# Layer 0's attention: latent before context, and two heads' value products in turn

## The chip, the core and the metric

The kernel runs as one program on one core of a Trainium2 chip. The time is that of the device, in microseconds (us): 2790.97 before the change, the median of three runs (2787.93 to 2791.73). TensorE (PE in the rows) multiplies matrices, VectorE (DVE) and ScalarE (ACT) do the elementwise work, and the queue of SyncE (SP) issues the transfers from the device's memory. Each engine takes its instructions in one fixed order that is set when the program is built.

## The reference, cut to what matters

The model is a trunk of four layers over 256 latent and 256 context tokens with 1024 features. Each layer has a token mixer and a squared-ReLU MLP. The change is in layer 0's mixer, multi-head latent attention with 16 heads. Keys and queries have 96 features per head, values 64:

```
q, k, v = project(u, True)          # 256 latent tokens
qc, kc, vc = project(uc, False)     # 256 context tokens
k_all = jnp.concatenate([k, kc], axis=2)
v_all = jnp.concatenate([v, vc], axis=2)
o  = softmax(q  k_all^T * scale) v_all     # latent queries see 512 keys
yc = softmax(qc kc^T    * scale) vc        # context queries see the 256 context keys
```

## The kernel before

The activations lie with features on partitions and 512 tokens (latent, then context) along the row. The function `mla_heads` works on heads in pairs, eight pairs one after another. The two heads of a pair fill the two halves of one output tile: head `e` = 0 goes to partitions 0 to 63 and head 1 to partitions 64 to 127 of `out`, a PSUM tile named `st`.

For one head there are four query tiles of 128 tokens: two latent ones that see 512 keys, and two context ones that see 256. One query tile is a *unit* in what follows:

- L864, TensorE: the score product `sc` = queries x keys.
- `softmax` (L664 to L667): VectorE takes the maximum (L664) and scales it (L665), ScalarE takes the exponential (L666), VectorE the reciprocal of the sum (L667).
- L868, VectorE: the probabilities `p` are scaled.
- L871, TensorE: `p` is transposed in blocks of 128 x 128 into `ax`.
- L879, VectorE and ScalarE: the transposed blocks are copied to `pt`, in which keys lie on partitions.

After its four units the head is multiplied with its values (L888): four products of 128 keys x 64 outputs x 256 latent queries, summed in one half of `out`, and then two for the context queries. All products of one head write the same half of the partitions; the other head's follow after its own four units. There are 16 x (4 + 2) = 96 such products. After both heads, `split` (L639, L640) cuts `out` into the two parts `uh` and `ul` that the output projection reads.

Between the units, `self.aside` takes steps of a generator: the projections of the next pair (`proj1` and `project`, whose products are L294 to L296 into `pj`), in the last pair the first products of the output projection (`early`). After each head, two steps of layer 0's modulation are made (`ada`, L432: four products with 32 output columns each, that write the four quarters of an `st` tile). The weights come through a ring of four buffers `raw` (L269 for weight blocks, L429 for the modulation), and ScalarE (L277) and VectorE (L278) split each weight block into `whi` and `wlo`.

The rows of buffers in `MLA_ROWS` give each kind of tile its ring: four buffers for `pt`. In which order instructions of one engine stand is settled by a scheduler when the program is built; a product in fp32 stands in the trace as two MATMUL records and two LDWEIGHTS records, a 128 x 128 transpose as one of each.

Of the kernel before, what the change touches and what calls it, by code (L numbers as in the profile page):

```python
# [12 lines left out]
F32 = mybir.dt.float32  # L13
# [8 lines left out]
S = 256  # L22
T2 = 512
# [19 lines left out]
MLA_ROWS = dict(q=4, k=4, p=4, pt=4, x=3)  # L43
# [4 lines left out]
class Cols:  # L48
    """Column layout of the packed per-feature parameters."""
# [19 lines left out]
def _wa(w, kc=8):  # L69
    """[K, F] -> [F/128, K/(128 kc), 128, kc * 128]: blocks that hold one tile of outputs."""  # L70
    k, f = w.shape
    w = w.reshape(k // (128 * kc), kc, 128, f // 128, 128)
    return np.ascontiguousarray(w.transpose(3, 0, 2, 1, 4)).reshape(f // 128, k // (128 * kc), 128, kc * 128)


def _wb(w):
    """[K, F] -> [F/512, K/256, 128, 2 * 512]: blocks that hold 512 outputs of 256 inputs."""
    k, f = w.shape
    w = w.reshape(k // 256, 2, 128, f // 512, 512)
    return np.ascontiguousarray(w.transpose(3, 0, 2, 1, 4)).reshape(f // 512, k // 256, 128, 1024)  # L80


def _rope(dim):
    """cos and signed sin of the axial positions: [128 features (whole heads), 256 tokens] each."""
# [10 lines left out]
def _layout(x):  # L95
    """Host side: arrays as the kernel reads them (transposed, cut and joined; no arithmetic)."""
# [40 lines left out]
    # rows 0-63 see (forward, backward) in the two passes over a token tile, rows 64-127 the other way round  # L137
# [18 lines left out]
class Trunk:  # L156
    def __init__(self, ctx, tc, ins, out):
        self.ctx, self.tc, self.nc, self.I, self.out = ctx, tc, tc.nc, ins, out
        # what a layer norm is cut into
# [32 lines left out]
    def open_acc(self, pool):  # L192
        """Banks for products in turn from a pool of two and from that for projections beside other work."""
        acc, pj = ("acc", pool("acc", 2, space=PSUM)), ("pj", self.pj)
        turn = cycle((acc, acc, pj, pj))

        def tile():
            n, p = next(turn)
            return p.tile([128, T2], F32, name=n)
        self.acc = tile  # L200

    def proj1(self, block, n=T2, kc=8, x=None, every=2):
        """As proj, for one block and from the pool for projections beside other work; yields after every few input tiles."""
# [20 lines left out]
    def after(self, ins, other):  # L224
        """ins comes after other, of the same engine."""
# [9 lines left out]
    def tables(self):  # L235
        """Loads the tables of exp and ln, both, after the last silu."""
# [5 lines left out]
    def weights(self, *key):  # L242
        """One block of weights, split; the blocks that come after it are loaded and split ahead."""
# [13 lines left out]
    def load(self, name, *at):  # L257
        """Loads one block of weights and splits it: hi + lo, both with at most 12 significant bits; some stay whole."""
# [13 lines left out]
    def halved(self, pool, src, n=""):  # L272
        """Up to 1024 columns from DRAM, split."""
# [7 lines left out]
    def blocks(self):  # L281
        """The blocks of weights in the order of their use."""
# [15 lines left out]
    def proj(self, blocks, n=T2, t0=0, kc=8, x=None, outer=None, spare=False):  # L298
        """Yields PSUM tiles [128 features, n tokens]; blocks: weight blocks, one per output tile.
        outer: output widths of blocks whose products go together, input tile by input tile.  # L300
        spare: the first product goes to another pool."""
# [32 lines left out]
    def ada_prepare(self):  # L334
# [3 lines left out]
        # stationary operands of 32 columns: both conditions, and sums of partitions into one column or the other  # L338
# [8 lines left out]
        # picks the streams' rows from each quarter, or their sums over the quarters  # L347
# [4 lines left out]
    def begin(self, raw, blocks):  # L352
        """The first sub-layer's input, tile by tile as its modulation arrives, and beside it the products with the
        first blocks of weights, which arrive between; returns those products."""
# [57 lines left out]
    def aside(self, n=None):  # L412
        """The next n steps of the modulation that is worked out beside other things."""
# [3 lines left out]
    def ada(self, i):  # L417
        """Modulation of layer i: mods[:, 8 * kind + tile, stream]; yields 8 times for each kind (begin makes the first two of
        layer 0).  The products of layer 0 are TensorE's, those of the others, which come beside an MLP, VectorE's."""
# [37 lines left out]
    def coef(self, i, sub, r):  # L457
        """u = n * A + B and the gate for layer i, sub-layer sub, stream r; n is -2 times the normalised stream, without gain."""
# [28 lines left out]
    def ln_add(self, d, a, b):  # L487
        """Takes columns a to b of tile d of z, complete (the first two tiles come with all their columns).
        Sums are about c, the mean of the features of the first two tiles; it is taken from the others beforehand."""
# [19 lines left out]
    def ln_finish(self, a, b):  # L509
        """Mean (of what is left of z) and -2 / deviation of columns a to b."""  # L510
# [11 lines left out]
    def rsqrt(self, out, x):  # L522
        """out = -2 (x + eps) ** -0.5: the tables' value and one Newton step; x is overwritten."""
# [15 lines left out]
    def coefs(self, i, sub, t=T2):  # L539
        """All that turns the normalised parts into the input of a sub-layer, and its gates."""  # L540
# [3 lines left out]
    def enter(self, sub, r):  # L544
        """u (split) and the residual of a sub-layer from stream r, normalised."""
# [21 lines left out]
    def last_tiles(self, blocks, x, kc, sub):  # L567
        """The last four output tiles before a layer norm, part by part: what follows it begins with one
        part while the other is still under way.  sub: what follows, or None at the end."""
# [22 lines left out]
    def last_part(self, sub):  # L592
        """What is left of a layer norm, to be made once the next sub-layer has begun."""
# [6 lines left out]
    def mlp(self, i, t, following=None):  # L600
        """following: makes the coefs of the sub-layer after it, which is entered."""
# [40 lines left out]
    def rsqrt_sum(self, out, s, n, t):  # L642
        """out = -2 (sum over partitions of s / n + eps) ** -0.5, on all partitions; s is overwritten."""
# [6 lines left out]
    def rope(self, x, swapped, tab, out):  # L650
        """x: [128, >= 256] in SBUF; swapped: scratch; out: list of (destination, partitions)."""
# [8 lines left out]
    def softmax(self, p, ps, n, scale):  # L660
        """p = exp(scale * ps - max); returns 1 / sum per partition."""
# [19 lines left out]
    def early(self, name, n=7):  # L681
        """The products of the first n input tiles with the first two blocks of an output projection."""
# [31 lines left out]
    # the order of the projections of the gated linear attention, after the first four  # L714
# [16 lines left out]
    # the order of the other projections of the gated delta rule, after the first keys  # L731
# [15 lines left out]
    def mixer0(self, i):  # L747
        nc, I = self.nc, self.I
        with ExitStack() as ctx:
# [9 lines left out]
            def gather(raw, blocks):  # L759
                """Copies of products and the sum of their squares."""  # L760
# [47 lines left out]
    def mla_heads(self, pool, vp, tab, cq, ck, kr):  # L808
# [7 lines left out]
        def project(quad):  # L816
            """Values of 4 heads, queries and keys of 2 pairs."""
# [32 lines left out]
        for pair in range(8):  # L850
# [6 lines left out]
            for e, (q, k) in enumerate(qk):  # L857
                hp = slice(64 * e, 64 * e + 64)
                pts = []
                for qt in range(4):  # L860
                    lat = qt < 2
                    k0, nk = (0, 4) if lat else (S, 2)
                    sc = self.sc.tile([128, T2], F32, name="sc")
                    nc.tensor.matmul(sc[:, :128 * nk], lhsT=q[0:96, 128 * qt:128 * qt + 128],  # L864
                                     rhs=k[0:96, k0:T2], start=True, stop=True)
                    p = row("p")
                    r = self.softmax(p, sc, 128 * nk, scale)
                    nc.vector.tensor_scalar_mul(p[:, :128 * nk], p[:, :128 * nk], r)  # L868
                    tp = self.ax.tile([128, T2], F32, name="ax")
                    for kt in range(nk):  # L870
                        nc.tensor.transpose(tp[:, 128 * kt:128 * kt + 128], p[:, 128 * kt:128 * kt + 128], self.ident)  # L871
                    if qt % 2 == 0:
                        pt = [row("pt") for _ in range(nk // 2)]
                        pts.append(pt)
                    # pt[j][:, kt % 2, query]
                    for j in range(nk // 2):
                        dst = pt[j].rearrange("p (k q) -> p k q", k=2)[:, :, 128 * (qt % 2):128 * (qt % 2) + 128]
                        src = tp[:, 256 * j:256 * j + 256].rearrange("p (k q) -> p k q", k=2)
                        (nc.scalar.copy if j else nc.vector.tensor_copy)(dst, src)  # L879
                    if pair == 7:  # L880
                        self.aside(2)
                    elif pair + 1 not in made:
                        self.aside(1 + pair % 2)
                h = 2 * (pair % 2) + e
# [983 lines left out]
```

## Time and profile before

| what | us |
|---|---|
| median of three runs | 2790.97 |
| lowest and highest run | 2787.93, 2791.73 |
| the profiled execution, first to last instruction | 2789.6 |
| TensorE busy | 2691.3 (96%) |
| VectorE busy | 2025.3 (73%) |
| ScalarE busy | 1255.1 (45%) |

The profiled execution is 1.4 us shorter than the median of the runs. A busy TensorE row counts the time in which at least one product is on its way; since products overlap, how long one holds the engine is read from the distance between the starts of two, not from its length.

### The profile page before, as it was taken

How to read it: one execution, taken by the hardware profiler on the slowest of the kernel's cores; microseconds unless marked ns; L12 is line 12 of the kernel's file. 1: busy time of each engine (PE TensorE's matmuls, PEld its weight loads, DVE VectorE, ACT ScalarE, POOL GpSimd, SP SyncE). 2: the span in 40 equal slices, each digit the busy share in tenths (PEclk: the TensorE clock that was granted, in tenths of full speed). 3: DMA queues.
4: the chain of work that ended last, by engine and by line, in shares of the span. 5: the costliest groups of instructions: out<-in, count | busy, mean ns of one | idle time of the engine just before them, and what ended most of it. 6: DMA issues, size and time to landing. Idle time of an engine off the chain costs nothing. (4 is left out here: it accounts for less than half of the span.)

```text
span 2789.6 us, 41018 instructions
## 1 busy us (share of the span) xinstructions
PE 2691.3 (96%) x15728; PEld 2166.6 (78%) x15728; DVE 2025.3 (73%) x3908; ACT 1255.1 (45%) x2413; POOL 47.9 (2%) x75
## 2 busy tenths in 40 slices
PE   7999999999999989999999999999999998998998
PEld 5666787788876687888888887887887876657997
DVE  3666798784757799875754489876689897668666
ACT  3544453333545663332454455322354555444544
POOL 0000000000000000000000000000000111000000
PEclk9999999999999999999999999999999898999999
DMA  6533237564121126654311125664322445313453
GB/s 232 174 97 104 78 106 218 180 191 134 59 69 50 34 79 218 197 175 147 93 63 56 58 76 178 199 189 159 117 82 81 158 153 151 107 29 121 159 182 113
DMA packets 125536, 353.26 MB, mean 127 GB/s; under 512 B 37499, under 2 KB 41339, under 8 KB 124828
## 3 DMA queue, kind: packets, MB, share of 16 engines
q1 hardware_dynamic: 121804, 337.00, 38.3%
q0 software_dynamic: 3536, 13.63, 1.3%
q8 instruction: 124, 2.03, 0.3%
q14 instruction: 72, 0.59, 0.1%
HBM read 335.91 MB, written 14.68 MB: 126 GB/s over the span
## 5 line engine op out<-in xcount | busy, mean ns | idle before, releaser
L277 ACT CAST whi<-raw 128x1024 fp32r<-128x1024 f32 (+2 forms) x403 | 410.4, 1023 | 694.0 <-PE acc L295 259.9
L278 DVE TENSOR_TENSOR wlo<-raw,whi 128x1024 fp32r<-128x1024 f32 (+2 forms) x403 | 478.0, 1189 | 199.7 <-ACT whi L277 193.9
L294 PE MATMUL pj<-ul,whi 128*128 128x512 f32 (+1 forms) x1072 | 398.6, 372 | 1.1 <-DVE z L565 1.0
L296 PE MATMUL pj<-uh,wlo 128*128 128x512 f32 (+1 forms) x1072 | 386.9, 361 | 0.6 <-DVE wlo L278 0.6
L295 PE MATMUL pj<-uh,whi 128*128 128x512 f32 (+1 forms) x1072 | 386.2, 360 | 0.0
L438 DVE SCALAR_TENSOR_TENSOR acc<-raw,s,acc 128x1024 f32<-128x1024 f32 x252 | 317.2, 1280 | 31.8 <-DMA raw<-in_ada 28.7
L294 PE MATMUL acc<-ul,whi 128*128 128x512 f32 (+3 forms) x888 | 311.7, 351 | 15.9 <-DVE ul L554 11.0
L295 PE MATMUL acc<-uh,whi 128*128 128x512 f32 (+3 forms) x888 | 308.7, 348 | 0.0
L296 PE MATMUL acc<-uh,wlo 128*128 128x512 f32 (+3 forms) x888 | 308.5, 347 | 0.0
L294 PEld LDWEIGHTS pj<-ul,whi 128*128 128x128 f32 x1072 | 203.0, 189 | 37.4 <-issue 6.3
L296 PEld LDWEIGHTS pj<-uh,wlo 128*128 128x128 f32 x1072 | 203.0, 189 | 32.6 <-issue 4.6
L295 PEld LDWEIGHTS pj<-uh,whi 128*128 128x128 f32 x1072 | 203.2, 190 | 30.1 <-issue 5.8
L294 PE MATMUL pj<-hl,whi 128*128 128x512 f32 (+1 forms) x560 | 198.3, 354 | 0.7 <-DVE hl L621 0.3
L294 PEld LDWEIGHTS acc<-ul,whi 128*128 128x128 f32 (+2 forms) x888 | 167.2, 188 | 40.6 <-DVE ul L554 12.9
L295 PE MATMUL acc<-hh,whi 128*128 128x512 f32 (+1 forms) x560 | 197.5, 353 | 0.0
L294 PE MATMUL acc<-hl,whi 128*128 128x512 f32 (+1 forms) x560 | 196.8, 351 | 0.0
L295 PE MATMUL pj<-hh,whi 128*128 128x512 f32 (+1 forms) x560 | 196.7, 351 | 0.0
L296 PE MATMUL acc<-hh,wlo 128*128 128x512 f32 (+1 forms) x560 | 196.5, 351 | 0.0
L296 PE MATMUL pj<-hh,wlo 128*128 128x512 f32 (+1 forms) x560 | 196.2, 350 | 0.0
L296 PEld LDWEIGHTS acc<-uh,wlo 128*128 128x128 f32 (+2 forms) x888 | 167.1, 188 | 22.1 <-issue 1.2
L295 PEld LDWEIGHTS acc<-uh,whi 128*128 128x128 f32 (+2 forms) x888 | 167.3, 188 | 20.8 <-issue 1.0
L620 ACT CAST hh<-t 128x512 fp32r<-128x512 f32 (+1 forms) x128 | 72.2, 567 | 123.6 <-DVE t L619 123.2
(463 smaller groups left out, 5001.0 us busy)
## 6 DMA issues: line engine op xcount, KB each, us to landing
raw<-in_w SPq DMA_DIRECT2D x256, 512.0 KB, 4.2
raw<-in_ada SPq DMA_DIRECT2D x192, 512.0 KB, 4.7
raw<-in_diff_qk SPq DMA_DIRECT2D x16, 512.0 KB, 3.5
raw<-in_gdn_v SPq DMA_DIRECT2D x16, 512.0 KB, 4.0
raw<-in_gdn_z SPq DMA_DIRECT2D x16, 512.0 KB, 4.5
raw<-in_gdn_out SPq DMA_DIRECT2D x16, 512.0 KB, 3.9
raw<-in_mla_in SPq DMA_DIRECT2D x9, 512.0 KB, 7.5
raw<-in_mla_qb SPq DMA_DIRECT2D x12, 384.0 KB, 3.6
```

The costliest lines, as they stand in the source:

```text
L277: nc.scalar.copy(hi[:, :width], raw[:, :width])
L278: nc.vector.tensor_sub(lo[:, :width], raw[:, :width], hi[:, :width].bitcast(F32))
L294: mm(ps, lhsT=ah, rhs=bl, start=start, stop=False)
L295: mm(ps, lhsT=ah, rhs=bh, start=False, stop=False)
L296: mm(ps, lhsT=al, rhs=bh, start=False, stop=stop)
L438: nc.vector.scalar_tensor_tensor(acc[r], w, self.s[:, k, r:r + 1], acc[r], op0=ALU.mult, op1=ALU.add)
L620: nc.scalar.copy(hh[:, f, :t], r[:, :t])
```

## The change

For each pair, the two latent query tiles of both heads are now taken first (query tile by query tile, both heads in turn), then the value products of both heads for the latent queries, then the same for the context. Within the value products, the key tiles follow each other, and for each key tile head 1 and head 0 are multiplied in turn. `pt` has six buffers in place of four, two per head for the latent and one for the context. Two steps of the modulation follow the latent and two the context, where two followed each head. Comments are left out as well, so that lines behind move: L871, L879 and L888 become L870, L875 and L884.

```
-MLA_ROWS = dict(q=4, k=4, p=4, pt=4, x=3)
+MLA_ROWS = dict(q=4, k=4, p=4, pt=6, x=3)
...
-            for e, (q, k) in enumerate(qk):
-                hp = slice(64 * e, 64 * e + 64)
-                pts = []
-                for qt in range(4):
-                    lat = qt < 2
-                    k0, nk = (0, 4) if lat else (S, 2)
...
-                h = 2 * (pair % 2) + e
-                for pt, o, t0 in ((pts[0], out[:, :S], 0), (pts[1], out[:, S:], 2)):
-                    nk = 2 * len(pt)
-                    for kt in range(nk):
-                        nc.tensor.matmul(o[hp], lhsT=v[:, t0 + kt, 64 * h:64 * h + 64],
-                                         rhs=pt[kt // 2][:, S * (kt % 2):S * (kt % 2) + S],
-                                         start=kt == 0, stop=kt == nk - 1)
+            for lat in (True, False):
+                k0, nk, t0, o = (0, 4, 0, out[:, :S]) if lat else (S, 2, 2, out[:, S:])
+                pts = [[row("pt") for _ in range(nk // 2)] for _ in qk]
+                for qt in range(2):
+                    qa = (0 if lat else S) + 128 * qt
+                    for (q, k), pt in zip(qk, pts):
...
+                for kt in range(nk):
+                    for e in (1, 0):
+                        h, pt = 2 * (pair % 2) + e, pts[e]
+                        nc.tensor.matmul(o[64 * e:64 * e + 64], lhsT=v[:, t0 + kt, 64 * h:64 * h + 64],
+                                         rhs=pt[kt // 2][:, S * (kt % 2):S * (kt % 2) + S], start=kt == 0, stop=kt == nk - 1)
                 for _ in islice(modulation, 2):
                     pass
```

In the built program the instructions are the same ones, and ahead of and behind this attention each engine's order is unchanged; the queues of SP and POOL are unchanged throughout. On TensorE 767 instructions in a row differ in their order. A first place is TensorE in the fourth pair, where the six value products of the first head stand before the change (`pt` and `v`: L888; `ident` and `p`: transposes; `raw` and `s`: the modulation):

```order
L888 MATMUL st<-pt,v 64x256 x2
L871 MATMUL ax<-ident,p 128x128 x2
L888 MATMUL st<-pt,v 64x256
L654 MATMUL ax<-x,swap 128x256
L888 MATMUL st<-pt,v 64x256 x3
L432 MATMUL st<-raw,s 32x256 x8
```

In the same pair after the change, TensorE has the latent products of both heads:

```order
L870 MATMUL ax<-ident,p 128x128 x4
L654 MATMUL ax<-x,swap 128x256
L296 MATMUL pj<-ck_132,wlo 128x512
L294 MATMUL pj<-cq_131,whi 128x512
L295 MATMUL pj<-cq_130,whi 128x512
L884 MATMUL st<-pt,v 64x256 x8
L432 MATMUL st<-raw,s 32x256 x8
L870 MATMUL ax<-ident,p 128x128 x2
```

Pieces of two, one and three products, all for the same half, became one piece of eight in which the halves alternate. A second place is ScalarE where two weight blocks of a later projection are split (`whi<-raw`), before the change:

```order
L879 COPY pt<-ax 128x2x128
L666 ACTIVATE p,sm<-sc,sm 128x256
L277 CAST whi<-raw 128x256
L666 ACTIVATE p,sm<-sc,sm 128x512
L277 CAST whi<-raw 128x768
L666 ACTIVATE p,sm<-sc,sm 128x512
```

And ScalarE at the same two weight blocks after the change:

```order
L666 ACTIVATE p,sm<-sc,sm 128x512
L666 ACTIVATE p,sm<-sc,sm 128x256
L277 CAST whi<-raw 128x256
L277 CAST whi<-raw 128x768
L875 COPY pt<-ax 128x2x128
L666 ACTIVATE p,sm<-sc,sm 128x256 x2
L447 COPY t_2181<-st 128x256
```

The two casts now stand next to each other, with a copy to `pt` and the exponentials of context units behind them.

## Rows read from the trace of the kernel before

**Rows 1.** The page: busy time, then busy tenths and granted clock in 40 slices.

```profile
PE 2691.3 (96%) x15728; PEld 2166.6 (78%) x15728; DVE 2025.3 (73%) x3908; ACT 1255.1 (45%) x2413; POOL 47.9 (2%) x75
...
PE   7999999999999989999999999999999998998998
...
PEclk9999999999999999999999999999999898999999
```

**Rows 2.** Busy time by stretches: all of this attention's changed order, then what follows.

```profile
core 0: us, PE busy (x) PEld busy (x) DVE busy (x) ACT busy (x) POOL busy (x), PEclk, DMA share, GB/s
123.70:326.20 202.50, 202.37 (x1015) 125.65 (x1013) 133.57 (x394) 92.93 (x233) 0.00 (x0) 1.00 0.30 95
...
326.20:420.00 93.80, 92.47 (x592) 81.39 (x592) 84.44 (x154) 51.86 (x93) 0.00 (x0) 1.00 0.32 101
```

**Rows 3.** Groups by line, 123.7 to 326.2 us: count, busy, mean, idle before.

```profile
L888 PE MATMUL st<-pt,v 128*64 128x256 f32 x192 | 50.6, 390 | 0.0
...
L871 PE MATMUL ax<-ident,p 128*128 128x128 f32 x192 | 31.8, 278 | 0.1
...
L888 PEld LDWEIGHTS st<-pt,v 128*64 128x64 f32 x192 | 22.7, 136 | 23.7 <-issue 7.4 <-DVE sm L665 2.2 <-DVE p L868 1.8
...
L277 ACT CAST whi<-raw 128x768 fp32r<-128x768 f32 (+3 forms) x24 | 18.6, 780 | 12.3 <-DMA raw<-in_mla_kb 8.7 <-PE pj L295 1.5 <-ACT p L666 1.2
```

**Rows 4.** Timeline of TensorE: start, length, records merged into pieces.

```profile
129.45 1.94 PE L888 MATMUL st<-pt,v 128*64 128x256 f32 x8
131.32 1.07 PE L432 MATMUL st<-raw,s 128*32 128x256 f32 x16
132.32 1.98 PE L864 MATMUL sc<-k,q 96*128 96x512 f32 x4
...
151.76 0.40 PE L296 MATMUL pj<-cq,wlo 128*128 128x512 f32 x1
151.99 0.40 PE L294 MATMUL pj<-cq,whi 128*128 128x512 f32 x1
...
152.46 0.40 PE L296 MATMUL pj<-cq,wlo 128*128 128x512 f32 x1
152.78 1.08 PE L888 MATMUL st<-pt,v 128*64 128x256 f32 x4
153.79 0.33 PE L871 MATMUL ax<-ident,p 128*128 128x128 f32 x1
```

**Rows 5.** Timeline of TensorE in layer 3, products whose two halves alternate.

```profile
2350.51 1.51 PE L1569 MATMUL acc<-S,kT 128*64 128x256 f32 x12
2352.03 1.26 PE L1581 MATMUL ax<-t,uc 128*128 128x128 f32 x8
```

**Rows 6.** Timeline of all engines: one latent unit from its score product to its transposes.

```profile
314.11 1.02 PE L864 MATMUL sc<-k,q 96*128 96x512 f32 x2
...
317.29 0.49 DVE L868 TENSOR_SCALAR p<-p,sm 128x512 f32<-128x512 f32 x1
...
317.95 0.38 PE L871 MATMUL ax<-ident,p 128*128 128x128 f32 x2
```

**Rows 7.** The same view: one context unit.

```profile
318.39 0.60 PE L864 MATMUL sc<-k,q 96*128 96x256 f32 x2
...
320.53 0.35 DVE L868 TENSOR_SCALAR p<-p,sm 128x256 f32<-128x256 f32 x1
```

**Rows 8.** Waits from 123.7 to 326.2 us: total, times, longest.

```profile
ACT p L666 <- DVE sm L665: 51.6, 26, 6.0
...
DVE sm L664 <- PE sc L864: 20.5, 20, 3.5
...
ACT whi L277 <- DMA raw<-in_mla_kb: 8.7, 3, 4.9
```

More of the change, by code (lines that the diff above doesn't have):

```diff
@@ L856, in mla_heads @@
             out = self.st.tile([128, T2], F32, name="st")
-            for e, (q, k) in enumerate(qk):
-                hp = slice(64 * e, 64 * e + 64)
-                pts = []
-                for qt in range(4):
-                    lat = qt < 2
-                    k0, nk = (0, 4) if lat else (S, 2)
[L863 to L869, printed above, removed]
-                    for kt in range(nk):
[L871 to L883, printed above, removed]
-                h = 2 * (pair % 2) + e
-                for pt, o, t0 in ((pts[0], out[:, :S], 0), (pts[1], out[:, S:], 2)):
-                    nk = 2 * len(pt)
-                    for kt in range(nk):
-                        nc.tensor.matmul(o[hp], lhsT=v[:, t0 + kt, 64 * h:64 * h + 64],
-                                         rhs=pt[kt // 2][:, S * (kt % 2):S * (kt % 2) + S],
-                                         start=kt == 0, stop=kt == nk - 1)
@@ new lines, in mla_heads @@
+            for lat in (True, False):
[4 more added lines that the diff above has]
+                    for (q, k), pt in zip(qk, pts):
+                        sc = self.sc.tile([128, T2], F32, name="sc")
+                        nc.tensor.matmul(sc[:, :128 * nk], lhsT=q[0:96, qa:qa + 128], rhs=k[0:96, k0:T2], start=True, stop=True)
+                        p = row("p")
+                        r = self.softmax(p, sc, 128 * nk, scale)
+                        nc.vector.tensor_scalar_mul(p[:, :128 * nk], p[:, :128 * nk], r)
+                        tp = self.ax.tile([128, T2], F32, name="ax")
+                        for kt in range(nk):
+                            nc.tensor.transpose(tp[:, 128 * kt:128 * kt + 128], p[:, 128 * kt:128 * kt + 128], self.ident)
+                        for j in range(nk // 2):
+                            dst = pt[j].rearrange("p (k q) -> p k q", k=2)[:, :, 128 * qt:128 * qt + 128]
+                            src = tp[:, 256 * j:256 * j + 256].rearrange("p (k q) -> p k q", k=2)
+                            (nc.scalar.copy if j else nc.vector.tensor_copy)(dst, src)
+                        if pair == 7:
+                            self.aside(2)
+                        elif pair + 1 not in made:
+                            self.aside(1 + pair % 2)
+                for kt in range(nk):
+                    for e in (1, 0):
+                        h, pt = 2 * (pair % 2) + e, pts[e]
+                        nc.tensor.matmul(o[64 * e:64 * e + 64], lhsT=v[:, t0 + kt, 64 * h:64 * h + 64],
+                                         rhs=pt[kt // 2][:, S * (kt % 2):S * (kt % 2) + S], start=kt == 0, stop=kt == nk - 1)
```

## The prediction

> **What bounds the kernel now.** I read the page first. TensorE is busy for 96% of the span, in nearly every slice, and its granted clock is 9 tenths or more in all slices but one [rows 1], so the whole program waits for TensorE almost everywhere. Then I cut out the stretch in which the change moves anything, 123.7 to 326.2 us: TensorE is busy for 202.37 of 202.50 us at a granted clock of 1.00, which is the 2.4 GHz level, VectorE for 133.57 and ScalarE for 92.93, and the DMA engines for 0.30 of the time [rows 2]. In this stretch the others wait for TensorE: VectorE's maximum waits 20.5 us for score products [rows 8], and neither the value products nor the transposes show more than 0.1 us of idle time ahead of them [rows 3]. A busy row can hide small waits, so I also laid the distances between starts along the built order: 0.23 us for a 512-column projection product, 0.12 for a 256-column one, 0.43 per record of a latent score product, 0.11 per transpose, and the figures below for the narrow products. They sum to 196.3 us of the 202.4, an estimate in which at most 6 us, 3%, are left for waits. So what TensorE saves here counts in full, until something else is late.
>
> **Term 1: the value products go in pairs.** The 192 records of L888 [rows 3] stand in 43 pieces, counted in the order. A piece of 8 records takes 131.32 - 129.45 = 1.87 us to the next start, a piece of 4 takes 153.79 - 152.78 = 1.01 [rows 4]. So a record costs (1.87 - 1.01) / 4 = 0.215, one after another, and a piece 1.01 - 4 x 0.215 = 0.15 on top. Before: 192 x 0.215 + 43 x 0.15 = 47.7 us.
>
> What do alternate halves do? L1569 in layer 3 has the same shape (128 rows, 64 columns, 256 moving columns, fp32), its halves alternate, and it writes both into one PSUM tile: 12 records take 2352.03 - 2350.51 = 1.52 us [rows 5]. One after another they would take 12 x 0.215 + 0.15 = 2.73; in six rounds of two, 1.44. The modulation's four quarters show the same: 16 records in 132.32 - 131.32 = 1.00 us [rows 4], four rounds of four (1.01) and not sixteen (3.59). So I take two at a time. After the change there are 18 pieces, each strictly alternating: 6 of eight products (16 records, 8 rounds, 1.87 us) and 12 of four (8 records, 4 rounds, 1.01 us), 23.3 us. **Saved: 24.4 us.**
>
> The Trainium skill speaks against this. "TensorE: Matmul & The Clock Gate", in Part 3 under "The mechanism", says that a weight load overlaps a running matmul only where the two use different row groups. These products use all 128 rows, in both halves. By that rule each load would stand alone. The trace disagrees already before the change: a load takes 0.136 [rows 3], and yet records with a load each follow at 0.215 in the piece of eight [rows 4], and rounds of two at about the same in layer 3 [rows 5]. By the rows term 1 is 24.4; by the rule it would be 96 rounds x 0.136 = 13.1 us less, 11.3.
>
> **Term 2: fewer changes of shape.** The step from a 128-column product into a piece of 64 columns costs 152.78 - 152.46 = 0.32 where the next product of the same shape would start after 0.23 [rows 4], so 0.09. 25 pieces fewer: **saved 2.2 us**. Leaving is in the 0.15 above.
>
> **Term 3: the modulation's pieces break more often.** L432 comes in groups of eight products, 4 rounds. Where the order cuts such a group, one of its sets of four starts anew and costs two more rounds. Before, four of ten groups are cut, after, seven of ten (as 1+7, 5+3, 3+5): 6 more rounds of 0.215, **lost 1.3 us**. Together 24.4 + 2.2 - 1.3 = 25.3 us less for TensorE, from 202.4 to about 177.
>
> **Term 4: waits that take their place.** A unit's transposes need its softmax. From score product to scaled probabilities that took 317.78 - 314.11 = 3.67 us in a latent unit [rows 6] and 320.88 - 318.39 = 2.49 in a context unit [rows 7]. TensorE fills this with other work, and the transposes wait in its queue at a place that the order fixes; behind them wait the projections that everything else needs. Laying the same distances along both orders, the work between a unit's score product and its first transpose shrinks: median 5.35 to 4.56 us for latent units, 4.7 to 4.25 for context units, and the very last context unit has only 1.1 us. With 4.2 and 3.2 us for a chain that meets a short queue on VectorE and ScalarE (half a microsecond or so over the two rows), the shortfalls sum to 3.1 us before and 8.5 after: **lost 5.4 us**. With the bare 3.7 and 2.5 it is 0.1 and 2.0, 1.9 lost; with a long queue (4.6 and 4.1), 16.1 and 23.6, so 7.5 lost. I take the middle since VectorE's load rises from 133.57 / 202.5 = 66% to some 73%, which is busy and not full.
>
> One more wait has no row for its new form. At four places in the order ScalarE's casts of two weight blocks now stand together, ahead of a copy to `pt` and of exponentials. Such casts waited 8.7 us for transfers, up to 4.9 at once [rows 3, 8], and cost TensorE nothing where much work was placed behind them. If none of it is covered now, up to 8.7 us more is lost; if covered as before, nothing. I count nothing, because the order still places some 6 us of work at the first context unit behind most of them, and keep 8.7 for the range.
>
> The rest is free. The two more `pt` buffers are space alone. `split` of a pair runs on ScalarE and VectorE while TensorE has the next pair's units; uncovered, it would cost about 1 us a pair. The transfers are the same in the same order, at 0.30 of the DMA time [rows 2]. Behind the stretch the order is unchanged and TensorE again bound (92.47 of 93.80) [rows 2], so the gain stays.
>
> **Sum.** 2789.6 - 25.3 + 5.4 = 2769.7 for the profiled execution. It was 1.4 under the median of the runs, so the time is 2771.
>
> **Rivals.**
>
> - *All of it arrives.* No new waits; the small waits of before stay. 2791 - 25 = 2766, and 2764 if the 3 us of waits before go too. For it: VectorE has room, and TensorE's queue lets later units catch up after one wait. Against: the shorter distances. 0.18.
> - *The softmax becomes the bound in stretches.* Both bounds of term 4 come together, 7.5 + 8.7 = 16.2 lost: 2791 - 25.3 + 16.2 = 2782. For it: the exponential's wait of 6.0 us for VectorE [rows 8], in-order queues, and eight units per pair now in two dense groups of four. Against: no idle time in the rows of before. 0.15 for 2776 to 2785.
> - *The pairs do not form.* Then only the fewer pieces count (25 x 0.24 = 6.0), against 1.3 and 5.4 lost: 2792, no change. For it: a half of L888's products has never met the other in this stage. Against: the same shape in layer 3 [rows 5]. 0.05.
> - *The pairs form, but each round waits for its weight load.* 13.1 us of the gain stay away: 2784. Against: the loads that are hidden now [rows 3 to 5]. 0.02. This is what the Trainium skill's rule on loads would make of the change.
> - *Slower.* The two casts hold up the copy to `pt`, so the value products, so the modulation's products behind them, which free the `raw` buffers for the very transfers that the casts wait for. If each of the 16 latent and context groups waits 2 us or more for this, 32 us, the gain of 25.3 is gone: at the longest wait seen, 4.9 us at eight of them and 5.4 elsewhere, 2791 - 25.3 + 39.2 + 5.4 = 2810. It decides from 1.6 us per group. For it: such waits stand in the rows. Against: only three in the whole stretch [rows 8]. 0.05.
>
> **How the numbers follow.** The forecast, 2767 to 2776 (terms 1 to 3 firm, term 4 between its bounds), has 0.55. Full gain 0.18, bound by the softmax 0.15, loads between rounds 0.02, no pairs 0.05, slower 0.05. A measurement of this kernel can tell 0.2%, 5.6 us, from no change. Faster by over that: 0.55 + 0.18 + 0.15 + 0.02 = 0.90; within it 0.05; slower 0.05. The range from 2764 to 2782 leaves out the last three cases and the end of the softmax's.
>
> **What would show it.** In the profile after, L884 has 192 records whose pieces of 16 take about 1.9 us and of 8 about 1.0. The stretch ends near 306 us and not 326. TensorE's idle time ahead of transposes (L870) rises from 0.1 to a few microseconds, named after VectorE's `p`; VectorE's and ScalarE's busy times stay as they were. If records of the two halves start 0.215 apart, term 1 is wrong; if the stretch shrinks by 15 us or less with paired records, term 4 is, and the waits of ScalarE's casts or of the copies to `pt` tell which half of it.

## The result, and the profile after

The changed kernel takes 2768.95 us (median of four runs, 2765.41 to 2770.39) against 2791.35 beside it: 0.9926 of the time before, 95% interval 0.9913 to 0.9938, 22 us or 0.74% faster. 2771 was forecast, with a range of 2764 to 2782.

The page of the profiled execution, which was the fastest of the four, answers to [rows 1]; the lines are the span, the busy time, and the granted clock in 40 slices:

```profile
span 2763.6 us, 41015 instructions
...
PE 2662.7 (96%) x15728; PEld 2155.1 (78%) x15728; DVE 2024.5 (73%) x3908; ACT 1251.8 (45%) x2413; POOL 48.3 (2%) x75
...
PEclk9999999999999999999999999999999898999999
```

The instruction counts of the engines and the row of the clock are as before. TensorE's busy row is 28.6 us shorter, that of the weight loads (PEld) 11.5, ScalarE's 3.3; VectorE's is the same within 1 us. The attention's changed order (the 202.50 us of [rows 2]) now runs from 122.0 to 303.1 us, in the view by stretches:

```profile
122.00:303.10 181.10, 177.12 (x1016) 115.77 (x1015) 132.95 (x395) 90.55 (x233) 0.00 (x0) 1.00 0.34 107
```

It is 21.4 us shorter. TensorE now stands idle for 181.10 - 177.12 = 4.0 us of it, where it was 0.1; VectorE is busy for 73% of it, the figure that term 4 named. Between the same two products ahead of the attention and behind it, which serve as marks for all kernels below, 244.6 us became 222.9. The view by stretches, before and after:

```profile
101.33:345.96 244.63, 242.11 (x1223) 156.29 (x1221) 169.38 (x460) 113.64 (x267) 0.00 (x0) 0.99 0.33 103
```

```profile
99.93:322.85 222.92, 216.57 (x1222) 146.11 (x1221) 168.49 (x460) 110.96 (x267) 0.00 (x0) 0.99 0.36 114
```

The granted clock of the marks is 0.99 in both. Two later executions of the changed kernel, at 1.00, took 221.7, about 1 us less. The other 4 us by which this execution is shorter came in stretches whose order didn't change: 1.4 ahead of the attention, the rest in layers 2 and 3, and there where the granted clock was higher than before (102.5 us at 0.98 became 101.1 at 1.00, 107.1 at 0.94 became 105.0 at 0.96). So I count the attention's 21.7 to the change and not the rest.

The groups by line in that stretch, which answer to [rows 3] (busy, mean, and idle time ahead with its releasers):

```profile
L870 PE MATMUL ax<-ident,p 128*128 128x128 f32 x192 | 31.6, 280 | 3.9 <-DVE p L867 3.9
...
L884 PE MATMUL st<-pt,v 128*64 128x256 f32 x192 | 24.7, 389 | 0.0
...
L277 ACT CAST whi<-raw 128x768 fp32r<-128x768 f32 (+3 forms) x24 | 18.7, 782 | 10.3 <-DMA raw<-in_mla_qb 6.0 <-PE sc L864 2.3 <-PE pj L295 1.6
```

The same 192 records keep the engine busy for 24.7 us where it was 50.6 with the same mean length of one: they overlap. And there is what the change brought with it, 3.9 us that TensorE waits for scaled probabilities ahead of its transposes. TensorE's timeline shows a piece of eight and one of four products, with what follows each:

```profile
130.71 1.95 PE L884 MATMUL st<-pt,v 128*64 128x256 f32 x16
132.59 0.66 PE L870 MATMUL ax<-ident,p 128*128 128x128 f32 x4
...
302.00 1.08 PE L884 MATMUL st<-pt,v 128*64 128x256 f32 x8
303.02 0.50 PE L294 MATMUL acc<-ul,whi 128*128 128x512 f32 x1
```

16 records take 132.59 - 130.71 = 1.88 us and 8 take 1.02: what 8 and 4 took in [rows 4]. The waits, which answer to [rows 8]:

```profile
ACT p L666 <- DVE sm L665: 39.5, 21, 4.3
...
DVE sm L664 <- PE sc L864: 14.6, 24, 1.1
...
ACT whi L277 <- DMA raw<-in_mla_qb: 6.0, 4, 2.5
```

These waits of ScalarE and VectorE shrank with the stretch, and casts wait less for transfers than before.

### The profile page after: what moved, and what is told of

Read it like the earlier page. It is cut to its first block, busy times and chain, and to the rows that moved or that the text cites. A ratio compares the mean times of both kernels' runs of the same rounds, so it can differ in the third digit from the quotient of the medians.

```text
span 2763.6 us, 41015 instructions
## 1 busy us (share of the span) xinstructions
PE 2662.7 (96%) x15728; PEld 2155.1 (78%) x15728; DVE 2024.5 (73%) x3908; ACT 1251.8 (45%) x2413; POOL 48.3 (2%) x75
```

## The experiments

**Jobs one and two.** Eight kernels; each was timed beside the kernel before. For each I also read four things from its profile: the length between the two marks, the sum of all pieces of value products (first start to the next other product), their count, and TensorE's idle time ahead of transposes. The granted clock between the marks stands behind their length; lengths at one clock are compared below where there are such.

| kernel | median us (ratio, interval) | marks (clock) | pieces: sum, count | idle ahead of transposes |
|---|---|---|---|---|
| before | 2788.25 and 2788.42 | 244.6 (0.99) | 47.73, 43 | 0.1 |
| changed | 2766.85 (0.9921, 0.9903 to 0.9939) | 221.7 (1.00) | 23.44, 18 | 3.8 |
| in series | 2775.34 (0.9955, 0.9940 to 0.9970) | 232.1 (1.00) | 31.31, 24 | 3.9 |
| products at the end | 2764.26 (0.9915, 0.9902 to 0.9927) | 219.4 (0.99) | 24.80, 23 | 0.6 |
| four buffers | 2767.95 (0.9924, 0.9912 to 0.9935) | 222.2 (1.00) | 23.44, 18 | 3.8 |
| products twice | 2787.30 (0.9993, 0.9985 to 1.0002) | 243.7 (0.99) | 44.17, 18 | 2.8 |
| one half | 2786.82 (0.9991, 0.9978 to 1.0004) | 242.2 (0.99) | 43.76, 16 | 2.2 |
| at the end, in blocks | 2772.18 (0.9939, 0.9919 to 0.9959) | 226.2 (1.00) | 32.17, 23 | 0.5 |
| context copies on ScalarE | 2765.28 (0.9917, 0.9899 to 0.9936) | 223.4 (0.99) | 23.45, 18 | 3.3 |

**In series.** Head 1's products first, then head 0's.

```
-                for kt in range(nk):
-                    for e in (1, 0):
+                for e in (1, 0):
+                    for kt in range(nk):
```

> The changed kernel with one edit: within the value products the two heads follow each other (all key tiles of head 1, then all of head 0) and don't alternate. The products, their buffers, and the order of units are those of the changed kernel (2769.0 us). Theory (the gain is that products of the two halves run two at a time, and only where neighbours in TensorE's order write different halves): nearly all 192 records stand one after another again, 96 more rounds of 0.215 us, and 24 pieces in place of 18, so the stretch of layer 0's attention is 17 to 22 us longer and the time 2786 to 2791, about that of the kernel before. Rival A (TensorE looks past the next product and runs a later one of the other half beside it): only the counts of each half in a piece matter, 16 rounds a pair in place of 12, 32 x 0.215 = 6.9 us, 2776. Rival B (the gain is the new order of units and the six buffers): no change, 2769.

Against the kernel with four buffers, in the same job, it lost 7 us of the gain by the runs and 10 between the marks, 7.9 of them in the pieces. That isn't all of it: nearest to rival A. TensorE's timeline shows how: two products of head 1 alone, then a piece of two more of head 1 and four of head 0.

```profile
128.59 1.08 PE L884 MATMUL st<-pt,v 128*64 128x256 f32 x4
129.60 0.62 PE L432 MATMUL st<-raw,s 128*32 128x256 f32 x4
130.16 1.95 PE L884 MATMUL st<-pt,v 128*64 128x256 f32 x12
132.04 0.66 PE L870 MATMUL ax<-ident,p 128*128 128x128 f32 x4
```

The 12 records take 1.88 us, the time of the eight of head 0. The single starts are 130.156, 130.169, 130.422, 130.436 and so on in twos, until four are left that start alone: records of one half start 0.215 apart, so the second must be head 0's, which runs beside head 1's first though three more records of head 1 stand between them in the order. My theory that only neighbours overlap was wrong.

**Products at the end.** The unit order of before, with six buffers and both heads' products at the end of the pair.

```
+            for e, (q, k) in enumerate(qk):
+                for qt in range(4):
...
+            for lat in (True, False):
+                nk, t0, o = (4, 0, out[:, :S]) if lat else (2, 2, out[:, S:])
+                for kt in range(nk):
+                    for e in (1, 0):
...
```

> The unit order of the kernel before (head by head, two latent and two context units each), but with the value products of both heads at the end of the pair, the halves in turn, and six buffers for the transposed probabilities. Theory (pairs of products are the gain, the order of units is not): 23 pieces, all alternating, 5 more than after the change (5 x 0.24 = 1.2 us); 2767 to 2774. Rival B (taking the latent of both heads first is what helps): most of the gain is lost, 2780 to 2791. If the products at the end of the pair come too late for what follows, waits ahead of them show it, and the time lies between.

The gain is all there, and between the marks 3 to 4 us more than with the change: 1.4 us more in pieces, but the idle time ahead of transposes is nearly gone, as the group of transposes by line shows:

```profile
L869 PE MATMUL ax<-ident,p 128*128 128x128 f32 x192 | 32.5, 279 | 0.6 <-DVE p L866 0.3
```

Taking the latent first isn't what gains.

**Four buffers.**

```
-MLA_ROWS = dict(q=4, k=4, p=4, pt=6, x=3)
+MLA_ROWS = dict(q=4, k=4, p=4, pt=4, x=3)
```

> The changed kernel with four buffers for the transposed probabilities in place of six (as before the change). TensorE's pieces are the same. Theory: the copies of the first context unit wait until the latent value products have read their buffers; a wait of VectorE of some 1 us per pair that TensorE's other work covers: 2767 to 2773. Rival B (the buffers are part of the gain): 2775 or more, with idle time ahead of the context copies.

No difference that the times or the marks can tell (222.2 against 221.7): the two buffers are no part of the gain.

**Products twice.**

```
+                for again in range(2):
+                  for kt in range(nk):
```

> The changed kernel with every value product made twice (the second time over the first, so the output stays). It doubles the disputed cost and nothing else. Theory: 96 products more in pairs are 96 rounds of 0.215 = 20.6 us, of which up to 3.6 us cover waits for the softmax that are there now: 2786 to 2790. If products of the two halves didn't overlap, it would be 192 records of 0.215 = 41 us: 2806 to 2811. If each round waited for its weight load (0.136 us), 33.7 us: 2799 to 2803.

2787.3, 19.4 us over the kernel with four buffers in the same job. The doubled pieces took 44.17 - 23.44 = 20.7 us more, 96 rounds of 0.216, and the idle time fell by 1.0.

**One half.** Nearly the same order (two pieces fewer), the pairs taken away.

```
+            nc.vector.memset(out[64:128], 0.0)
...
-                        nc.tensor.matmul(o[64 * e:64 * e + 64], lhsT=v[:, t0 + kt, 64 * h:64 * h + 64],
-                                         rhs=pt[kt // 2][:, S * (kt % 2):S * (kt % 2) + S], start=kt == 0, stop=kt == nk - 1)
+                        nc.tensor.matmul(o[0:64], lhsT=v[:, t0 + kt, 64 * h:64 * h + 64],
+                                         rhs=pt[kt // 2][:, S * (kt % 2):S * (kt % 2) + S], start=kt == 0 and e == 1, stop=kt == nk - 1 and e == 0)
```

> The changed kernel, its order and its pieces, but both heads' products go to the same half of the output tile, summed; the other half is set to zero by VectorE (the output is then not the reference's: heads are added up). It takes away nothing but the second half. Theory: no two products overlap, 192 records stand one after another, 96 more rounds of 0.215 = 20.6 us, less the up to 3.9 us of waits that this covers: 17 to 21 us over the changed kernel, 2784 to 2790. Rival B (the order of units and the denser pieces are the gain): within 3 us of the changed kernel.

Nearly the whole gain is lost by this alone, 20.0 us. Its timeline for the piece that took 1.88 us in the changed kernel:

```profile
133.95 3.67 PE L885 MATMUL st<-pt,v 128*64 128x256 f32 x16
137.55 0.66 PE L871 MATMUL ax<-ident,p 128*128 128x128 f32 x4
```

16 records one after another, 3.60 us. What this kernel keeps of the gain, 2.4 us between the marks, is about that of fewer pieces (4.0) less the waits (2.1).

Both heads' products are also added to one sum here, so this kernel alone leaves open whether the half or the sum has to differ. The kernel before settles it: its piece of 8 records in [rows 4] is, in the built order, the last two latent and both context products of head 0, two sums in one half, and it took 1.87 us, one record after another. It is the half.

**At the end, in blocks.** Products at the end, heads not in turn.

```
-                for kt in range(nk):
-                    for e in (1, 0):
+                for e in (1, 0):
+                    for kt in range(nk):
```

> The products at the end of the pair, all of head 1 and then all of head 0, in place of in turn. After the products in series, theory A is now that TensorE starts a later product of the other half beside an earlier one when both stand in one piece: a piece costs the records of the half that has more. Counted over its 23 pieces that is 126 rounds where the products in turn have 96: 30 x 0.215 = 6.5 us over the products at the end in turn (2764.3): 2769 to 2773. If only direct neighbours overlapped, nearly 80 rounds more, 17 us: 2779 to 2783.

The time fits, 2772.2, but the counting behind it doesn't. Where two of each head stand together (8 records) the piece takes about 1.03 us, as in turn, and where four of each do, much more:

```profile
269.08 1.09 PE L883 MATMUL st<-pt,v 128*64 128x256 f32 x8
270.11 0.66 PE L869 MATMUL ax<-ident,p 128*128 128x128 f32 x4
...
286.17 2.86 PE L883 MATMUL st<-pt,v 128*64 128x256 f32 x16
288.96 0.44 PE L869 MATMUL ax<-ident,p 128*128 128x128 f32 x2
```

The second is 2.79 us, not the 1.88 that the larger half alone would need, nor 3.60. In another piece, four products of head 1 and three of head 0, four records start alone, 0.22 apart, and the first of head 0 starts with the fifth (135.757 and 135.763); four alone and then eight rounds are 12 x 0.215 + 0.15 = 2.73, about what the piece above takes. So TensorE reaches past some products but not past all. The starts in every piece with both halves, in this kernel and in the one in series, fit the same reach: the first record of head 0 passes three records of head 1, whether four of them stand ahead of it or eight.

**Context copies on ScalarE.**

```
-                            (nc.scalar.copy if j else nc.vector.tensor_copy)(dst, src)
+                            (nc.scalar.copy if j or not lat else nc.vector.tensor_copy)(dst, src)
```

> The changed kernel with the context units' copies of transposed probabilities on ScalarE in place of VectorE (32 copies of 0.42 us). Theory: what TensorE waits for after the change, 3.9 us in five places, is VectorE's queue ahead of the scaled probabilities; with 13 us less on VectorE these waits shrink to 0 to 2 us, 1 to 4 us faster than the changed kernel beside it. Rival: the exponentials on ScalarE are as often the late part; then the copies ahead of them make the waits longer, 0 to 4 us slower.

Its stretch between the marks, at the same granted clock as the changed kernel's row above:

```profile
100.22:323.63 223.41, 217.28 (x1222) 145.68 (x1221) 157.75 (x428) 120.66 (x299) 0.00 (x0) 0.99 0.36 114
```

VectorE is busy for 10.7 us less, ScalarE for 9.7 more. The waits hardly moved, 3.3 us where 0 to 2 were expected, and the length didn't shrink (222.9 in the changed kernel). The theory fell: VectorE's load alone doesn't make the waits. What VectorE's load does by itself isn't shown, since ScalarE had more to do at the same time. Where the waits stand in the changed kernel says more. One of the three longest, in its timeline of all engines, is a context unit's:

```profile
160.46 0.60 PE L864 MATMUL sc<-k,q 96*128 96x256 f32 x2
...
161.11 0.83 ACT L277 CAST whi<-raw 128x768 fp32r<-128x768 f32 x1 [2.33 <-PE sc L864]
...
161.85 1.17 ACT L840 COPY q<-pj 64x512 f32<-64x512 f32 x2
162.00 0.15 DVE L665 TENSOR_SCALAR sm<-sm 128x1 f32<-128x1 f32 x1
...
162.82 1.05 PE L432 MATMUL st<-raw,s 128*32 128x256 f32 x10
163.04 0.47 ACT L666 ACTIVATE p<-sc,sm 128x256 f32<-128x256 f32 x1
...
163.84 0.42 DVE L841 COPY q<-x 32x512 f32<-32x512 f32 x1
164.29 0.35 DVE L867 TENSOR_SCALAR p<-p,sm 128x256 f32<-128x256 f32 x1
...
164.79 0.41 PE L870 MATMUL ax<-ident,p 128*128 128x128 f32 x2 [0.92 <-DVE p L867]
```

The exponential was due at 162.15 and came at 163.04, behind a cast and two copies on ScalarE; the scaling of the probabilities then stood behind a copy on VectorE. So this chain took 4.18 us, 1.7 more than the bare one of [rows 7], and TensorE, which had 3.4 us of work (until 163.87), ran dry. Another wait, of 1.07 us, has the same form. The largest, 1.34 us, is that of the very last context unit:

```profile
298.33 0.60 PE L864 MATMUL sc<-k,q 96*128 96x256 f32 x2
...
299.23 0.40 PE L296 MATMUL acc<-uh,wlo 128*128 128x512 f32 x1
...
300.47 0.35 DVE L867 TENSOR_SCALAR p<-p,sm 128x256 f32<-128x256 f32 x1
...
300.97 0.41 PE L870 MATMUL ax<-ident,p 128*128 128x128 f32 x2 [1.34 <-DVE p L867]
```

Its chain is a bare one, 300.82 - 298.33 = 2.49 us, and TensorE had only 1.3 us of work.

**Job three.** So I took the shortfall against a bare softmax (3.7 and 2.5 us, [rows 6, 7]) as the theory, and tried the changed kernel's unit order with the products at the end:

```
+            made_pts = {}
             for lat in (True, False):
...
+            for lat in (True, False):
+                nk, t0, o = (4, 0, out[:, :S]) if lat else (2, 2, out[:, S:])
                 for kt in range(nk):
...
```

> The unit order of the changed kernel (latent of both heads, then context), but the value products of both at the end of the pair, halves in turn. Theory: a wait arises where the order puts less work between a unit's score product and its first transpose than a bare softmax takes (3.7 us latent, 2.5 us context). Laid along the orders with the distances of the profile, that shortfall is 0 to 0.1 us before the change, 1.6 to 2.3 after it, 0.1 to 0.3 with head-by-head units and products at the end, and 0.2 to 0.4 here. So TensorE's waits for scaled probabilities fall from 3.9 to under 1 us; 24 pieces in place of 18 cost 1.4 us: the attention stretch is 1 to 3 us shorter than the changed kernel's, 2763 to 2767. Rival: taking the latent of both heads first brings the waits (dense groups for VectorE), wherever the products stand; 3 to 4 us of waits stay and the stretch is 1 to 3 us longer than the changed kernel's, 2768 to 2771.

> The kernel with head-by-head units and the products of both heads at the end of the pair once more, beside the changed kernel in one job. Theory: 2 to 4 us faster than the changed kernel, since its waits for scaled probabilities are gone (0.3 us) and its product pieces are only five more. Rival: within 1 us of it, the earlier difference was one of jobs.

> The changed kernel beside the two others: 2765 to 2770, waits for scaled probabilities 3.9 us.

Latent first, products at the end: 2761.20 (0.9906, 0.9885 to 0.9927), 219.4 us between the marks. Its group of transposes:

```profile
L871 PE MATMUL ax<-ident,p 128*128 128x128 f32 x192 | 31.6, 279 | 0.9
```

No wait for scaled probabilities is left among those listed, and the idle time is 0.9 us in scraps of at most 0.14. Head by head, products at the end: 2763.22 (0.9913, 0.9891 to 0.9934), 218.5. Changed: 2763.66 (0.9911, 0.9892 to 0.9930), 221.7, waits 3.7. These three lengths, all at a granted clock of 1.00, say that either version with the products at the end is 2 to 3 us faster in the attention. The whole times don't say it: their intervals cover each other, and runs of one kernel lay up to 15 us apart in this job, with their granted clock (2775.2 at 0.981 and 2760.5 at 0.987, head by head). A version that beats the change is therefore shown for the stretch and not for the whole.

In job two the changed kernel itself was the measure:

> The changed kernel itself, beside the others of this job. All theories: 2765 to 2770, its attention stretch as in its first profile, with 3.9 us of TensorE's waits for scaled probabilities.

2766.85; marks 221.7, waits 3.8.

## Why the prediction was right

**What bounds the kernel.** Right. TensorE's savings came through to the end nearly one for one, and nothing behind the attention became late.

**Term 1, the pairs.** Right, in its size too: the pieces were said to go from 47.7 to 23.3 us, and went from 47.73 to 23.45. That it is the two halves and nothing else is shown by the kernel with one half (20 us lost), the one with the products twice (20.7 us for 96 rounds), and the two sums in one half that don't overlap. The objection from the Trainium skill, that weight loads of the same rows don't overlap a running product ("TensorE: Matmul & The Clock Gate", Part 3, "The mechanism"), doesn't hold here: 192 records in 23.45 us leave no time for 96 loads of 0.136 between rounds. The products made twice say it too: had each round waited for its load, they would have cost 33.7 us more, and they cost 20.7.

**Terms 2 and 3, fewer pieces and broken modulation groups.** 0.9 us together was forecast. Between the marks 21.7 us were gained, the pieces gave 24.3 and the new idle time took 3.8, so 1.2 is left for these two. The modulation's pieces in the two traces tell them apart: a whole group takes 1.00 us, one cut as 5 + 3 products 0.98 + 0.56, and without the waits they sum to about 1.1 us more than before, where term 3 took 1.3. That leaves 2.3 for the fewer changes of shape, an estimate by subtraction, where term 2 took 2.2.

**Term 4, the waits.** The mechanism was right and its size too large: 3.9 us of idle time, where 5.4 was taken and 1.9 to 7.5 allowed. This is the term that makes up most of the 2 us by which 2771 was high. The distances were laid rightly: in the trace after, the work beside a unit's chain is 4.7 us for latent and 4.5 for context units in the median, where 4.56 and 4.25 were laid. I had chosen the middle because VectorE is busy for 73%. That reason failed: with 10.7 us less of its work the waits stayed.

The theory of job three, that the shortfall against a bare softmax decides, holds for one wait only. Read off the traces and not laid along the orders, that shortfall is 0 before the change, 1.2 after it, all of it in the last context unit, and 0 with the products at the end. The other 2.6 us stand where TensorE had 3.4 to 5.3 us of work, more than a bare chain takes, and the chain took 4.2 to 5.5 behind other work on ScalarE and VectorE: the queue that term 4 had put at half a microsecond or so. With the products at the end, head by head, the work between a context unit's score product and its transposes is even shorter (median 3.7 us, 4.5 in the changed kernel), and yet the waits are nearly gone, because the chains are shorter too (3.5 and 4.0). That either kernel of job three would wait for less than 1 us was forecast rightly, for a reason that covers less than half of what was saved. Why the queues ahead of the chains are shorter there wasn't tried.

**The wait that had no row.** Two casts in a row on ScalarE ahead of a copy and exponentials were given up to 8.7 us and counted at nothing. The waits that are put down to transfers are now 6.0 us, 2.5 at the longest, and TensorE shows no idle time of its own for them; one of its waits for the softmax stands behind such a cast, whose own 2.33 us the view puts down to a score product (in the rows of that wait above).

**The sums.** Two don't come out of their terms: 2764 for the full gain without the 3 us of waits is 2791 - 25.3 - 3.1 = 2763, and the 2776 at the upper end of the forecast lies 3 us above what term 4's longest queue gives, 2791 - 25.3 + 7.5 = 2773. Neither decides anything here.

**The rivals.** That all of it arrives is refuted by 3.9 us of idle time, that the softmax becomes the bound by how little that is. That pairs don't form, and that each round waits for its load, are refuted by the pieces. For the loop of waits that would make it slower there is no sign: the casts wait less than before.

## What to carry to other kernels

Two fp32 products of 64 output columns each that write different halves of the partitions cost TensorE one product's time (0.216 us a round, 0.215 a record alone) if they stand together in its order, so work for the two halves should be brought together, even where their inputs are ready at different times. What that costs is a wait wherever the chain on the other engines takes longer than the work that the order puts beside it. Both have to be looked at: the bare chain against the work finds the one unit at the end that has too little beside it, but most of the waits here came from chains that other work on ScalarE and VectorE held up, and those are only seen with the queues laid out. Putting the value products at the end of the pair took most of both away in this kernel; that is shown for the attention's stretch.

## What the runs showed of the hardware that had not been expected

TensorE doesn't hold strictly to its order of products: in the kernel in series, a record of the second half started 0.013 us after the first one of the other half and ahead of three that stood before it in the program. It didn't reach past seven: with eight records of one half ahead, four ran alone first, and 16 records took 2.79 us where 1.88 in turn and 3.60 in one half were measured. In all 32 pieces of the two kernels that hold both halves the starts fit a reach of three records. How far it reaches in other forms of product, and what sets the reach, wasn't tried.
